# Sparse attention's paired score products in one chain, two PSUM banks at a time, and both sums of values behind all scores

## The chip, the cores and the metric

The kernel runs on one core of a Trainium2 chip. The metric is the device time of one execution in microseconds (us), the median of several runs. TensorE (PE) multiplies matrices, VectorE (DVE) and ScalarE (ACT) work on elements and empty PSUM, GpSimd (POOL) does a little, and SyncE (SP) issues the transfers.

## The reference, cut to what matters

One layer of a streaming encoder block over 256 frames of 1024 channels: a combined input projection, two attention branches, gates, an output projection, a residual sum, a mixture of experts, a norm. The branch that the change touches is the sparse attention: an indexer picks 64 keys for each query, and attention runs over these. The kernel computes the scores over all keys and adds a bias of -1e30 where a key was not picked.

```python
def indexed_sparse_attention(q, k, v, q_idx, k_idx, w_idx, top_k):
    ...
    score = jnp.einsum('bqh,bqhk->bqk', wi, jax.nn.relu(logits))
    _, sel = lax.top_k(jnp.where(adm[None], score, -jnp.inf), top_k)
    k_sel, v_sel = gather(k, sel), gather(v, sel)
    s = jnp.einsum('bqhd,bqkhd->bhqk', qi, k_sel) * (DSA_HEAD_DIM ** -0.5)
    p = jax.nn.softmax(jnp.where(sel_ok[:, None], s, NEG), axis=-1)
    return jnp.einsum('bhqk,bqkhd->bqhd', p, v_sel)
```

Eight heads of 64 channels; queries in two blocks of 128 (`j` = 0, 1), with 128 and 256 keys.

## The kernel before

Every fp32 product is made of three products of fp32r halves (`hi`, `lo`): `mm3` (L301 to L303) for operands that fill 128 rows, `mm3_pair` (L318) for operands of 64 rows. `mm3_pair` is given two sets of operands, one in partitions 0 to 63 and one in partitions 64 to 127, and issues them by turns, each into a bank of its own.

The work comes in stages. The input projections and the indexer fill the first 118 us or so; `select` (L473) is the indexer's score, which uses `mm3_pair` too. Then come the attention branches, as generators that are advanced by hand (`steps`): `attend` for the latent attention and `attend_pairs` (L604) for the sparse one, in two quads of four heads, `B[0]` and `B[1]`. One advance of `attend_pairs` is one block of queries: two banks of scores are taken from `psS`, each is opened by a product that adds the bias (L615) and gets six products (L318) from each of two heads' halves; then, bank by bank, the row maximum (DVE L623), the exponentials (ACT L629), a reciprocal and a scaling (DVE L632, L634), transposes on PE (L640) and a copy into `PT` (ACT L642, L644). The third advance sums the values: 16 products (L652) into one bank of `psS`, and its evacuation by ACT L291 and DVE L294 into `obT`.

`psS` has two banks in all; each `pss()` takes the one that comes free. `psA` (four banks) holds the projections, `psT` (two banks) the transposes.

The order in which an engine runs its instructions is worked out when the kernel is built, by a planner that simulates all engines with a table of costs and takes, of what is ready, what has the highest priority. `steps` raises the priority of the attention's instructions by 400 places. Beside them stand the gates' and output projections, `project_late` (L725): 4 slabs' worth of splits into halves (`split_late`, ACT L282 or L297 and DVE L283 or L297) and the products L301 to L303 on them. `halves` holds four split parts. `after(i, j)` adds an edge to the planner: `i` comes behind `j` in the program of their engine. It makes no instruction.

Weights come by `issue` (L215) in SP's queue, attention slabs (`w_att`) through a ring of four places, and expert slabs (`w_moe`, 96 of 1 MB) into every place that has come free, such as those of `PT`, of `vb` and of `obT`. The experts begin with a gather (L895) and `gate_up` (L1047) and take the slabs in order; a slab's place is loaded again when its products are done.

Of the kernel before, what the change touches and what calls it, by code (L numbers as in the profile page):

```python
# [78 lines left out]
def block_kernel(ctx: ExitStack, tc: tile.TileContext, a, out, cap=CAP):  # L79
    nc = tc.nc  # L80
# [9 lines left out]
    def after(i, j):  # L90
        tc.add_manual_dep(i.ins, j.ins.name, nosync, reason="the latter goes first")
# [15 lines left out]
    def at(place, shape, dt=F32R, name="r"):  # L107
        n = int(np.prod(shape[1:]))
        t = rp.tile([128, 2048], dt, tag=place,
                    name=name)  # L110
        return shaped(t[:, :n], shape)
# [6 lines left out]
    def pt(name="t", which=None):  # L118

        if which is None:  # L120
            which = t_turn[0] = 1 - t_turn[0]
        return psT.tile([128, 512], F32, tag=f"t{which}", name=name)

    def pss(name="s"):
        return psS.tile([128, 512], F32, tag="s", name=name)

    def bc(ap, n, axis=1):

        p, m = ap.shape
        return ap[:, None, :].to_broadcast([p, n, m]) if axis == 1 else ap[:, :, None].to_broadcast([p, m, n])  # L130
# [37 lines left out]
    ident_r = cp.tile([128, 128], F32R, name="ident_r")  # L168
# [121 lines left out]
    def evac(hi, lo, ps, place=None):  # L290
        i = nc.scalar.copy(hi, ps)  # L291
        if place:
            first[place] = i.ins
        return i, nc.vector.tensor_sub(lo, ps, hi.bitcast(F32))  # L294
# [16 lines left out]

    row_halves = slice(0, 64), slice(64, 128)

    def mm3_pair(both, start, stop):

        for l, r, s0, s1 in ((1, 3, start, False), (1, 4, False, False), (2, 3, False, stop)):
            for ops in both:
                nc.tensor.matmul(ops[0], ops[l], ops[r], start=s0, stop=s1)  # L318

    scr_turn = [0]  # L320

# [113 lines left out]
    bias = wk.tile([128, 2, 256], F32R, tag="b3", name="bias", bufs=1)  # L435
# [37 lines left out]
    def select(j):  # L473

        nk = 128 * (j + 1)
        per = 512 // nk
        qs = slice(j * 128, (j + 1) * 128)
        sc = e0[:, 1664:1920] if j else e0[:, 1536:1664]
        for h0 in range(0, 4, per):
            p = [pss() for _ in range(2)]  # L480
            for i in range(per):
                mm3_pair([(p[z][:, i * nk:(i + 1) * nk], qiT[ps_, 0, h0 + i, qs], qiT[ps_, 1, h0 + i, qs],
                           kiT[ps_, 0, :nk], kiT[ps_, 1, :nk]) for z, ps_ in enumerate(row_halves)], True, True)
            for z in range(2):
                rl = wk.tile([128, 512], F32, tag="b2", name="rl", bufs=3)
                nc.scalar.activation(rl, p[z], AF.Relu)
                for i in range(per):
                    h = 4 * z + h0 + i
                    nc.vector.scalar_tensor_tensor(sc, rl[:, i * nk:(i + 1) * nk], wi[:, j, h:h + 1],
                                                   adm[:, 256 - nk:] if h == 0 else sc, op0=ALU.mult, op1=ALU.add)  # L490
        for r in range(TOPK // 8):
            m8 = wk.tile([128, 8], F32, tag="m8", name="m8")
            nc.vector.max(out=m8, in_=sc)
            nc.vector.match_replace(out=sc, in_to_replace=m8, in_values=sc, imm_value=TAKEN)
        nc.vector.tensor_scalar(bias[:, j, :nk], sc, -2e38, NEG, op0=ALU.is_gt, op1=ALU.mult)
# [66 lines left out]
    def attend(quad, scores, v, oT, op):  # L562
# [38 lines left out]
        evac(oT[:, 0, 2 * quad:2 * quad + 2], oT[:, 1, 2 * quad:2 * quad + 2], o.rearrange("p (c q) -> p c q", c=2), op)  # L601
        yield

    def attend_pairs(quad, v, oT, op):  # L604


        turn[0] = 1 - turn[0]
        place = f"T{turn[0]}"
        PT = at(place, [128, 4, 3, 128], F32)
        for j in range(2):  # L610
            nk = 128 * (j + 1)
            qs = slice(j * 128, (j + 1) * 128)
            p = [pss()[:, :2 * nk] for _ in range(2)]
            for z in range(2):
                nc.tensor.matmul(p[z].rearrange("p (h k) -> p h k", h=2), ident_r, bc(bias[:, j, :nk], 2), start=True,  # L615
                                 stop=False)
            for i in range(2):
                h = 2 * quad + i
                mm3_pair([(p[z][:, i * nk:(i + 1) * nk], qbT[r, 0, h, qs], qbT[r, 1, h, qs], kbT[r, 0, h, :nk],
                           kbT[r, 1, h, :nk]) for z, r in enumerate(row_halves)], False, i == 1)  # L620
            for z in range(2):
                nm = wk.tile([128, 4], F32, tag="nm", name="nm")[:, :2]
                nc.vector.tensor_reduce(nm, p[z].rearrange("p (h k) -> p h k", h=2), axis=AX.X, op=ALU.max, negate=True)  # L623
                if j or not z:
                    P = wk.tile([128, 512], F32, tag="b2", name="P", bufs=3)
                Pz = P[:, 256 * z:256 * z + 256] if j == 0 else P
                sm = wk.tile([128, 4], F32, tag="sm", name="sm")[:, :2]
                for i in range(2):
                    nc.scalar.activation(Pz[:, i * nk:(i + 1) * nk], p[z][:, i * nk:(i + 1) * nk], AF.Exp,  # L629
                                         bias=nm[:, i:i + 1], scale=1.0, accum_out=sm[:, i:i + 1])  # L630
                rs = wk.tile([128, 4], F32, tag="rs", name="rs")[:, :2]
                nc.vector.reciprocal(rs, sm)  # L632
                for i in range(2):
                    nc.vector.tensor_scalar(Pz[:, i * nk:(i + 1) * nk], Pz[:, i * nk:(i + 1) * nk], rs[:, i:i + 1], None,  # L634
                                            op0=ALU.mult)
                if z == 0 or j:
                    tp = pt()
                for b in range(2 * (j + 1)):
                    c = 256 * z + 128 * b if j == 0 else 128 * b
                    nc.tensor.transpose(tp[:, c:c + 128], P[:, c:c + 128], ident)  # L640
                if j:
                    nc.scalar.copy(PT[:, 2 * z:2 * z + 2, 1:3], tp.rearrange("p (h b q) -> p h b q", h=2, b=2))  # L642
                elif z:
                    first[place] = nc.scalar.copy(PT[:, :, 0], tp.rearrange("p (h q) -> p h q", h=4)).ins  # L644
            yield
        o = pss("o")
        for c in range(2):
            for b in range(2):
                for i in range(2):
                    r = slice(64 * i, 64 * i + 64)  # L650
                    h = 2 * quad + 4 * c + i
                    nc.tensor.matmul(o[r, c * 256 + 128 * b:(c + 1) * 256], v[:, b, 64 * h:64 * h + 64],  # L652
                                     PT[:, 2 * c + i, 0:2] if b == 0 else PT[:, 2 * c + i, 2], start=b == 0, stop=b == 1)
        evac(oT[:, 0, quad::2], oT[:, 1, quad::2], o.rearrange("p (c q) -> p c q", c=2), op)
        yield

    def steps(g, n):
        with tc.high_priority(400):
            for _ in range(n):
                next(g, None)  # L660
# [47 lines left out]
    qbT = at("C0", [128, 2, 4, S])  # L708
# [5 lines left out]
    kbT = at("C1", [128, 2, 4, S])  # L714
    dsa_heads(acc, kbT, 0, "C1")
    steps(A[1], 1)
    obT = at("C1", [128, 2, 4, S])
    B = [attend_pairs(quad, vb, obT, "C1") for quad in range(2)]
    steps(B[0], 2)
    steps(B[1], 1)  # L720
    steps(B[0], 1)
    steps(B[1], 2)


    def project_late(nslabs, lhs, banks, g=None):  # L725
# [446 lines left out]
    with in_order, tc.manual_schedule(engines={mybir.EngineType.Activation, mybir.EngineType.DVE}):  # L1172
        for grp in range(NG):
# [26 lines left out]
            if grp + 1 < NG:  # L1200
                for c in range(2):
                    p = pss("gx")
# [128 lines left out]
```

## Time and profile before

| | us |
|---|---|
| median of 3 runs | 427.56 |
| lowest, highest | 427.43, 428.58 |
| profiled execution, its own time | 428.7 |
| profiled execution, span of the instructions | 426.9 |

The span runs from the first to the last instruction of the profiled execution; 1.8 us of its time lie outside. In a timeline an instruction's duration runs to its modelled end, so that pipelined products overlap and the distance between two starts is what each costs. The mean granted clock of TensorE over the span is 0.972 of its upper level, 2.4 GHz.

### The profile page before, as it was taken

What the parts mean: (1) busy time and instruction counts of PE and PEld (TensorE: products, weight loads), DVE (VectorE), ACT (ScalarE), POOL (GpSimd) and SP (SyncE); (2) the same over time, 40 slices, a digit from 0 to 9 for tenths busy, and PEclk for the clock granted to TensorE, in tenths of its full rate; (3) what the DMA queues carried; (4) which work ended last, traced back from release to release, by engine and by line L of the source; (5) the groups of instructions that cost most, each with busy time, mean ns of one, the idle gap of its engine ahead of it and who ended that gap; (6) DMA issues with size and microseconds to landing.
All of it is one profiled execution on the core that took longest, in us unless ns stands there. A gap on an engine that the chain in (4) does not pass through costs nothing.

```text
span 426.9 us, 8162 instructions
## 1 busy us (share of the span) xinstructions
PE 400.3 (94%) x3288; PEld 292.6 (69%) x3288; DVE 205.8 (48%) x546; ACT 185.2 (43%) x403; POOL 27.7 (6%) x30
## 2 busy tenths in 40 slices
PE   7999999999999999999999999999999797788780
PEld 4888887888877787888886757575757373364440
DVE  2889689989857474757572222121213011020023
ACT  3876688578856665565442122221221111111142
POOL 0890000000000000000001010101010001000000
PEclk9999999999999999999999999999999889698996
DMA  7995673648553464978885999999999999999962
GB/s 264 395 338 194 256 296 129 264 164 332 198 188 128 161 253 176 378 284 341 334 321 184 418 421 421 421 418 420 420 421 419 421 419 421 422 418 420 417 253 104
DMA packets 20639, 135.00 MB, mean 316 GB/s; under 512 B 2418, under 2 KB 2930, under 8 KB 5620
## 3 DMA queue, kind: packets, MB, share of 16 engines
q1 hardware_dynamic: 20596, 134.42, 79.3%
q8 instruction: 28, 0.46, 0.4%
q14 instruction: 15, 0.12, 0.1%
HBM read 133.36 MB, written 1.05 MB: 315 GB/s over the span
## 4 chain that ended last, share of the span: by engine, by line
PE 77%; DMA 19%; DVE 2%; issue 0%; ACT 0%; SPq 0%; DVEq 0%
DMA w<-in_w_moe 18%; PE a L301 13%; PE a L302 13%; PE a L303 13%; PE G L1047 9%; PE gx L895 5%; PE Y L1088 5%; PE OA L1102 3%; PE G L1063 3%; PE s L318 2%; PE o L599 1%; DMA x<-in_x 1%; PE t L640 1%; PE t L539 1%; PE o L652 1%; PE t L451 1%
## 5 line engine op out<-in xcount | busy, mean ns | idle before, releaser
L302 PE MATMUL a<-r 128*128 128x512 f32 (+1 forms) x244 | 93.9, 387 | 0.0
L303 PE MATMUL a<-r 128*128 128x512 f32 (+1 forms) x244 | 92.1, 383 | 0.0
L301 PE MATMUL a<-r 128*128 128x512 f32 (+1 forms) x244 | 84.6, 390 | 0.0
L1047 PE MATMUL G<-w,tok 128*32 128x256 f32 x1024 | 71.2, 406 | 11.6 <-DMA w<-in_w_moe 11.4
L297 DVE SCALAR_TENSOR_TENSOR r<-w,ident,r 128x512 fp32r<-128x512 f32 (+2 forms) x79 | 62.4, 803 | 13.1 <-ACT r L297 12.7
L297 ACT ACTIVATE r<-w,ident 128x512 fp32r<-128x512 f32 (+2 forms) x79 | 57.0, 751 | 24.5 <-PE a L303 22.7
L1047 PEld LDWEIGHTS G<-w,tok 128*32 128x32 f32 x1024 | 30.0, 114 | 38.8 <-issue 15.8
L302 PEld LDWEIGHTS a<-r 128*128 128x128 f32 x244 | 45.9, 188 | 8.7 <-DVE r L297 0.3
L301 PEld LDWEIGHTS a<-r 128*128 128x128 f32 x244 | 45.4, 189 | 9.3 <-ACT r L291 0.5
L303 PEld LDWEIGHTS a<-r 128*128 128x128 f32 x244 | 45.8, 188 | 8.1
L1069 DVE TENSOR_TENSOR P<-G,P 128x64 f32<-128x64 f32 x32 | 7.2, 225 | 82.9 <-ACT P L1068 82.9
L1068 ACT ACTIVATE P<-G 128x64 f32<-128x64 f32 x32 | 7.2, 224 | 73.6 <-PE G L1063 73.6
L1088 PE MATMUL Y<-w,P 128*32 128x256 f32 x512 | 31.0, 382 | 2.2 <-DMA w<-in_w_moe 2.2
L1053 ACT COPY Gs<-G 128x256 f32<-128x256 f32 x32 | 11.9, 372 | 48.8 <-PE G L1047 48.8
L895 PEld LDWEIGHTS gx<-Pr,x 128*128 128x128 f32 x256 | 29.2, 192 | 3.3 <-issue 2.9
L297 DVE SCALAR_TENSOR_TENSOR ysb<-Y,ws,ysb 128x512 fp32r<-128x512 f32 (+1 forms) x18 | 12.5, 692 | 38.8 <-ACT ysb L297 19.6
L895 PE MATMUL gx<-Pr,x 128*128 128x128 f32 x256 | 30.7, 278 | 0.2 <-DVE Pr L880 0.2
L283 DVE TENSOR_TENSOR r<-w,r 128x512 fp32r<-128x512 f32 x32 | 21.9, 690 | 17.3 <-ACT r L282 15.7
L880 POOL TENSOR_SCALAR Pr<-P,r 128x128 f32<-128x128 f32 x14 | 8.3, 606 | 320.2 <-PE gx L895 195.1
L282 ACT CAST r<-w 128x512 fp32r<-128x512 f32 x32 | 19.8, 622 | 15.0 <-PE a L303 8.3
L1063 PEld LDWEIGHTS G<-cst,Gs 128*128 128x128 f32 x128 | 17.5, 199 | 9.8 <-issue 5.3
L1088 PEld LDWEIGHTS Y<-w,P 128*32 128x32 f32 x512 | 15.1, 109 | 12.6 <-DMA w<-in_w_moe 2.5
(223 smaller groups left out, 463.0 us busy)
## 6 DMA issues: line engine op xcount, KB each, us to landing
w<-in_w_moe SPq DMA_DIRECT2D x93, 1024.0 KB, 19.8
w<-in_w_att SPq DMA_DIRECT2D x24, 1024.0 KB, 4.9
w<-in_w_moe SPq DMA_DIRECT2D x6, 512.0 KB, 15.0
w<-in_w_att SPq DMA_DIRECT2D x3, 744.0 KB, 8.4
w<-in_w_att SPq DMA_DIRECT2D x2, 512.0 KB, 5.3
out<-r SPq DMA_DIRECT2D x2, 512.0 KB, 3.5
w<-in_w_att SPq DMA_DIRECT2D x1, 768.0 KB, 6.0
w<-in_w_att SPq DMA_DIRECT2D x2, 372.0 KB, 6.0
```

Of the source, the lines that this page charges most:

```text
L282: nc.scalar.copy(hi, src)
L283: nc.vector.tensor_sub(lo, src, hi.bitcast(F32))
L297: return nc.scalar.mul(hi, ps, g), nc.vector.scalar_tensor_tensor(lo, ps, g, hi.bitcast(F32), op0=ALU.mult, op1=ALU.subtract)
L301: i = nc.tensor.matmul(out_, lh, rh, start=start, stop=False)
L302: nc.tensor.matmul(out_, lh, rl, start=False, stop=False)
L303: nc.tensor.matmul(out_, ll, rh, start=False, stop=stop)
L895: nc.tensor.matmul(p[:, kk * GRP:(kk + 1) * GRP], x2[:, t, k * 128:(k + 1) * 128], Pr[:, t], start=(t == 0 and kk == 0), stop=(t == 1 and ...
L1047: nc.tensor.matmul(G[quarters[2 * z + o], :256], tokens[c][:, kk + o, CAP * e:CAP * e + CAP], w[:, (kk + o) * 512 + z * 256:(kk + o) * 512 ...
L1053: nc.scalar.copy(Gs, G[:, :256])
L1063: nc.tensor.matmul(HT[:, f * 64:(f + 1) * 64], Gs[:, f * 128:(f + 1) * 128], fold, start=True, stop=True)
L1088: nc.tensor.matmul(Y[quarters[e]], hT_[:, e, f], wv[:, f, e], start=f == 0, stop=f == 1)
L1102: nc.tensor.matmul(OA[t][h][:, c0:c0 + w], pl[:, t * 128:(t + 1) * 128], v, start=False, stop=grp == NG - 1 and q0 > 0 and v is lo, skip_g ...
```

## The change

`mm3_pair` puts each product that it issues behind the one before, and returns the last. In `attend_pairs` the first of these is put behind the second bank's bias product, the second head's products behind the first head's, and a pair's first bias product behind the last product of the pair before (`paired`). `select` calls `mm3_pair` without a start, so there the six products of one call are chained among themselves. The advances of the two quads are put into another order: before B0, B0, B1, B0 (sum), B1, B1 (sum), after B0, B0, B1, B1, B0 (sum), B1 (sum).

```diff
-    def mm3_pair(both, start, stop):
+    def mm3_pair(both, start, stop, behind=None):
 
         for l, r, s0, s1 in ((1, 3, start, False), (1, 4, False, False), (2, 3, False, stop)):
             for ops in both:
-                nc.tensor.matmul(ops[0], ops[l], ops[r], start=s0, stop=s1)
+                i = nc.tensor.matmul(ops[0], ops[l], ops[r], start=s0, stop=s1)
+                if behind:
+                    after(i, behind)
+                behind = i
+        return behind
...
+    paired = []
+
     def attend_pairs(quad, v, oT, op):
...
             for z in range(2):
-                nc.tensor.matmul(p[z].rearrange("p (h k) -> p h k", h=2), ident_r, bc(bias[:, j, :nk], 2), start=True,
-                                 stop=False)
+                i_ = nc.tensor.matmul(p[z].rearrange("p (h k) -> p h k", h=2), ident_r, bc(bias[:, j, :nk], 2), start=True,
+                                      stop=False)
+                if not z and paired:
+                    after(i_, paired.pop())
             for i in range(2):
                 h = 2 * quad + i
-                mm3_pair([(p[z][:, i * nk:(i + 1) * nk], qbT[r, 0, h, qs], qbT[r, 1, h, qs], kbT[r, 0, h, :nk],
-                           kbT[r, 1, h, :nk]) for z, r in enumerate(row_halves)], False, i == 1)
+                i_ = mm3_pair([(p[z][:, i * nk:(i + 1) * nk], qbT[r, 0, h, qs], qbT[r, 1, h, qs], kbT[r, 0, h, :nk],
+                           kbT[r, 1, h, :nk]) for z, r in enumerate(row_halves)], False, i == 1, i_)
+            paired.append(i_)
...
     steps(B[0], 2)
+    steps(B[1], 2)
+    steps(B[0], 1)
     steps(B[1], 1)
-    steps(B[0], 1)
-    steps(B[1], 2)
```

## Rows read from the trace of the kernel before

**Rows 1.** The page of the profile: busy time of the engines (us, share of the span, instructions), and two lines of the span in 40 equal slices (PE busy in tenths, DMA engines busy in tenths).

```profile
PE 400.3 (94%) x3288; PEld 292.6 (69%) x3288; DVE 205.8 (48%) x546; ACT 185.2 (43%) x403; POOL 27.7 (6%) x30
...
PE   7999999999999999999999999999999797788780
...
DMA  7995673648553464978885999999999999999962
```

**Rows 2.** Stretches of the span: the stretch and its length in us, busy us (and instructions) of PE, of weight loads, DVE, ACT and POOL, the granted clock of TensorE, the busy share of the DMA engines, GB/s.

```profile
150.00:160.00 10.00, 10.00 (x49) 8.10 (x48) 7.72 (x15) 6.51 (x13) 0.00 (x0) 1.00 0.65 242
160.00:170.00 10.00, 9.98 (x54) 7.14 (x53) 4.51 (x7) 6.30 (x10) 0.00 (x0) 1.00 0.51 181
188.00:222.00 34.00, 34.00 (x187) 28.93 (x186) 22.66 (x61) 17.27 (x35) 0.00 (x0) 1.00 0.92 356
222.00:228.00 6.00, 5.84 (x61) 4.79 (x63) 4.44 (x22) 1.10 (x6) 1.21 (x2) 1.00 0.05 19
...
230.00:328.00 98.00, 98.00 (x1244) 66.59 (x1247) 20.64 (x59) 20.82 (x55) 4.75 (x8) 1.00 1.01 418
328.00:407.00 79.00, 65.25 (x696) 38.46 (x684) 10.28 (x29) 12.55 (x32) 2.38 (x4) 0.89 1.01 419
```

**Rows 3.** The chain that ended last, in order of time, from 320 us to the end: start, us, what.

```profile
328.45 19.94 DMA w<-in_w_moe
...
388.24 18.66 DMA w<-in_w_moe
```

**Rows 4.** Waits of SP's queue between 160 and 245 us: who waited for whom, us in total, times, the longest.

```profile
SPq L215 <- PE G L1047: 18.7, 7, 11.7
...
SPq L215 <- PE o L652: 6.6, 1, 6.6
```

**Rows 5.** The chain over the whole span, its paired products in `select`: start, us from the first start to what comes next, count.

```profile
59.76 1.26 PE s L318 x20
65.56 0.91 PE s L318 x12
```

**Rows 6.** The chain between 118 and 170 us, the same products in `attend_pairs`.

```profile
124.24 0.81 PE s L318 x6
126.29 0.81 PE s L318 x6
...
129.38 0.91 PE s L318 x6
...
131.36 0.91 PE s L318 x6
137.82 0.81 PE s L318 x6
139.02 0.81 PE s L318 x6
...
147.03 0.79 PE s L318 x5
...
154.47 0.90 PE s L318 x6
```

**Rows 7.** Timeline of PE, the borders of such blocks: start, us to the modelled end, line, operation, tiles and shape, count.

```profile
128.76 0.39 PE L303 MATMUL a<-r 128*128 128x512 f32 x1
128.98 0.40 PE L615 MATMUL s<-bias,ident_r 128*128 128x512 f32 x1
129.31 0.98 PE L318 MATMUL s<-r 64*128 64x256 f32 x6
...
132.20 0.50 PE L302 MATMUL a<-r 128*128 128x512 f32 x1
132.54 0.40 PE L303 MATMUL a<-r 128*128 128x512 f32 x1
132.78 0.39 PE L302 MATMUL a<-r 128*128 128x512 f32 x1
...
145.86 0.49 PE L615 MATMUL s<-bias,ident_r 128*128 128x512 f32 x1
146.28 0.38 PE L318 MATMUL s<-r 64*128 64x256 f32 x1
146.59 0.44 PE L652 MATMUL o<-r 128*64 128x128 f32 x4
146.96 0.86 PE L318 MATMUL s<-r 64*128 64x256 f32 x5
```

**Rows 8.** Timeline of DVE and of ACT between 124 and 146 us, the softmax of the bank whose products end at 132.27: its row maximum, and the last of its exponentials.

```profile
132.31 0.69 DVE L623 TENSOR_REDUCE nm<-s 128x2 f32<-128x512 f32 x1 [0.15 <-PE s L318]
...
134.58 0.46 ACT L629 ACTIVATE P<-s,nm 128x256 f32<-128x256 f32 x1
```

**Rows 9.** Waits of all engines between 110 and 235 us, one row: ACT's splits of weights waiting for PE.

```profile
ACT r L297 <- PE a L303: 10.0, 15, 1.4
```

**Rows 10.** Timeline of ACT between 168 and 187 us: the evacuation of the last sum of values, and the first split of the slab that is multiplied with `obT`.

```profile
168.69 0.59 ACT L291 CAST r<-o 128x512 fp32r<-128x512 f32 x1 [0.52 <-PE o L652]
...
181.46 0.62 ACT L282 CAST r<-w 128x512 fp32r<-128x512 f32 x1 [0.33 <-PE a L303]
```

**Rows 11.** Timeline of SP's queue, two issues behind the last sum of values.

```profile
168.68 0.33 SPq L215 DMA_DIRECT2D w<-in_w_moe  x1
169.11 0.38 SPq L215 DMA_DIRECT2D w<-in_w_att  x1
```

## Prediction, written before the changed kernel was run

> **What bounds the kernel now.** I read the page first. PE is busy for 94% of the span, in tenths 9 in nearly every slice to about 330 us; the DMA engines are half idle until about 220 us and full from there to 410 us [rows 1]. An average over two such halves says little, so I cut the span into stretches [rows 2]. Up to 222 us PE is never free: 10.00 of 10 us, 34.00 of 34. From 230 us the DMA engines are at 1.01 and move 418 GB/s, while PE is full to 328 us and then only 65 of 79 us. The chain that ended last says the same of the end: from 328.45 to 406.90 us it consists of expert slabs' transfers [rows 3].
>
> The kernel is thus bound by PE first and by the transfers afterwards, and what couples the two decides what a gain on PE is worth. Between 222 and 228 us the DMA engines do almost nothing (share 0.05) [rows 2], and SP's queue stands in its longest wait of that part, 11.7 us, for the first `gate_up` products, L1047 [rows 4]. All places are full then; the stream of expert slabs starts again only when PE has used up the first of them. From that moment nothing but bytes stands between it and the end. So a microsecond that PE saves before 222 us starts the stream a microsecond earlier and ends the kernel a microsecond earlier, as long as the prefetch before is done in time. It has slack: it ends about 6 us ahead of the restart, and is busy for 0.92 of 188 to 222 us and 0.51 to 0.65 of 150 to 170 us [rows 2].
>
> The change works between 118 and 170 us, on PE's bound side.
>
> **Pairing.** Two places of the trace show the same products in two orders. In `select` the two row halves alternate: 12 products of 256 columns take 0.91 us, 20 of 128 columns 1.26 us [rows 5]. In `attend_pairs` they don't: each bank is opened by its own bias product, gets its six products, and the other bank follows 1 to 8 us later, with other work between. There six products of 256 columns take 0.91 us and six of 128 columns 0.81 us [rows 6]. Twelve alternating products cost what six of one half cost, so the two halves of the array work at once when they are fed by turns. For 128 columns the same follows from the steps: 20 products are 10 steps in 1.26 us, six of one half are 6 steps in 0.81 us, a step is (1.26 - 0.81) / 4 = 0.11 us, and 12 alternating products, 6 steps, take 0.81 us. The chain of the change forces the turns: z = 0, z = 1, z = 0, and so on, behind both bias products. Each of the four pairs of blocks then becomes one block, and the second of each goes: 0.81 + 0.91 + 0.81 + 0.90 = 3.43 us [rows 6].
>
> **Borders.** A block of 64-row products costs something on entry and exit. A full product starts 0.22 to 0.24 us after the one before, but from the bias product at 128.98 to the block behind it are 0.33 us, and from the first product behind a block, 132.20, to the next are 0.34 us [rows 7]. That is 0.10 us at each border, and four blocks fewer make eight borders fewer: 0.8 us.
>
> **The split block.** B1's first 256-column block was cut: one product at 146.28, four sums of values at 146.59, then the other five [rows 7]. Its first product alone takes 0.31 us, against 0.11 us for a step in a block; with the sums traced behind all scores this cut has no reason to happen: 0.2 us. The other sums are moved, not removed; their price is the same wherever they stand, and I take nothing for them.
>
> **The chain in `select`.** The six products of a call get edges in the order that they already show: its blocks of 20 and 12 run at the paired price [rows 5]. I take nothing; if one more cut came in or one went, it would be two borders, 0.2 us either way. The edges make no instructions.
>
> **What can be lost.** The planner may put other work between the links of a chain. Transposes of an earlier bank (L640) have the priority of earlier work and can become due in the middle of a pair. Such a cut costs two borders and perhaps a lone product, 0.2 to 0.4 us; with none to two in each pair it is 0 to 3.2 us. Blocks in the trace are mostly whole (seven of eight) [rows 6], so I take one cut in all, 0.2 us.
>
> **The waits that are added.** A pair now needs both banks of `psS` at its start. A bank is free when its softmax has read it: for the block that ends at 132.27 us the row maximum starts at 132.31 and the last exponential ends at 135.04 us [rows 8], 2.8 us. In PE's queue stands, behind a pair that waits, everything else of PE. What hides this is the projections: between the blocks that end at 132.27 and begin at 137.82 us [rows 6] PE had products L301 to L303 to do, and these are enough for any place that the planner chooses. I cost it at nothing, with an upper end of 2.8 us for each of the three pairs that follow another, 8.4 us, if nothing were put between.
>
> Behind this stands a second cover. Two softmaxes now come in one burst, and ACT and DVE also split the weights for PE. ACT waited for PE 15 times, 10.0 us in all, with its next split [rows 9], so it runs ahead. Four split parts are kept, each worth six products of 0.23 us, 1.4 us: 5.5 us of cover against a burst of about 2.8 us. Nothing, again; without that cover PE would miss the difference of the burst, at most 2.8 us a pair.
>
> One rule of the Trainium skill speaks against the change here: TensorEngine Tiling (Array Packing), section Performance Considerations, says that tiling speeds up TensorE but not the emptying of PSUM, which can become the bottleneck. By that rule the pairs would come no faster than the 2.8 us of the softmax let them; by the rows that price is covered, and the sum stands.
>
> **What is late next.** The sums of values move behind all scores. B0's sum, in part at 146.59 us before [rows 7], comes later; `PT`'s place then takes an expert slab later. B1's scores end earlier, since its last block no longer waits for B0's sum to leave a bank, so `obT` should not be later than now: it is evacuated from 168.69 us, and the slab that is multiplied with it is split from 181.46 us [rows 10], a slack of 12 us. On SP's queue a slab of attention weights can stand behind an expert slab that waits for a place. It did before: the queue waited 6.6 us for L652 [rows 4], the attention slab behind followed at 169.11 us [rows 11], and PE was still busy for 9.98 of those 10 us [rows 2]. So I cost the moved issues at nothing.
>
> **The sum.** 3.43 + 0.8 + 0.2 - 0.2 = 4.2 us off PE's stage, all of it before 170 us, and passed on whole. Span 426.9 - 4.2 = 422.7; with the 1.8 us outside it, 424.5 for an execution like the profiled one (428.7). That one lies 1.1 us above the median of the runs, so the forecast for the median is 427.56 - 4.2 = 423.4 us. Its own range is 422.6 to 424.5.
>
> **Rivals.**
>
> *Cuts.* The pairs are alternated, but transposes and sums break them up, or the two bias products and the pair stand apart. One or two cuts a pair of 0.2 to 0.4 us leave 1.6 to 3 us of gain: 424.6 to 426.0. For it: the cut block at 146.28, and that edges don't forbid other work between. Against it: seven whole blocks of eight, and 20 and 12 in one piece in `select`. Chance 0.18.
>
> *Order elsewhere.* The planner's later order changes for the better beyond my sum, such as fewer cuts of the sums of values: 421 to 422.5. Chance 0.04.
>
> *Nothing arrives.* PE waits for second banks or splits about 1.4 us before each of three pairs and loses what it gains, or the change's edges don't keep the turns on the chip: 427.6, within 0.3%. For it: the planner's costs aren't the chip's, and PE takes its queue in order. Against: no stretch between 118 and 222 us shows PE free [rows 2]. Chance 0.12.
>
> *Slower.* The banks. The planner puts a pair directly where its simulation has both banks free, the chip frees the second up to 2.8 us later, and PE stands with all projections behind it. Three times 2.8 us less the gain of 4.2 us is 4.2 us slower: 431.8. It decides from a mean wait of 1.4 us before the three pairs. For it: both banks of `psS` are in every pair, so no bank is left to work ahead in; against it: softmax times are regular, and PE met no such wait with the same two banks before. Chance 0.11. By the skill page named above this is the case to expect whenever evacuation is the slower side; the trace agrees only in that 2.8 us are more than the 0.9 us of a block.
>
> **From these to the numbers.** The forecast has 0.55. From no change, a measurement of this kernel can tell about 0.3%, 1.3 us. Faster by more: 0.55 + 0.18 + 0.04 = 0.77; within: 0.12; slower: 0.11. The range leaves out the slower case, about half of the case without change and half of the large gains, 0.19 in all: 421.8 to 427.4.
>
> **What would show it.** In the changed trace, L318 in four blocks of 12, 0.81 us for 128 columns and 0.91 us for 256, each behind two bias products; no idle PE before L615 or L318; the restart of the expert stream behind L1047 about 4 us earlier than 228 us, with DMA share 1.01 after it; the last expert transfer at about 402.7 instead of 406.90 us. Blocks of 4 or 8 with other lines between would be the first rival, PE idle before L615 the last. The forecast is wrong in its coupling if PE's stage is 4 us shorter and the stream's restart or its length doesn't follow.

## The result, and the profile after

The changed kernel takes 423.26 us, the median of 4 runs (422.87 to 424.31), against 427.94 us (427.43 to 428.58) for the kernel before beside it: a ratio of 0.9893, 95% interval 0.987 to 0.9915, or 3.6 to 5.6 us off. The forecast was 423.4 us. A second series of the same kernel gave 424.01 us and 0.9916 (0.9889 to 0.9942). The profiled execution took 422.87 us with a span of 421.1 us.

The page of the changed kernel, its lines for busy time and for the DMA engines over the span:

```profile
PE 391.6 (93%) x3288; PEld 287.8 (68%) x3288; DVE 205.3 (49%) x546; ACT 184.1 (44%) x403; POOL 27.0 (6%) x30
...
DMA  7995673748544489679867999999999999999962
```

Against [rows 1] PE has as many products and is busy for 8.7 us less; that is more than the change gains, for it counts the start and the end too, where the two executions differ (65.25 against 63.65 us in the last row of the two tables of stretches). Stretches of the span in which the work is about that of [rows 2], each some 4 us earlier (columns as there):

```profile
184.00:218.00 34.00, 33.89 (x188) 28.53 (x186) 23.42 (x67) 16.07 (x32) 0.00 (x0) 1.00 0.90 341
218.00:224.00 6.00, 5.96 (x73) 4.88 (x77) 3.41 (x16) 1.29 (x7) 1.21 (x2) 1.00 0.16 37
226.00:324.00 98.00, 98.00 (x1238) 66.56 (x1235) 20.64 (x59) 20.74 (x55) 4.75 (x8) 1.00 1.01 421
324.00:403.00 79.00, 63.65 (x701) 37.69 (x699) 10.45 (x31) 12.55 (x34) 2.38 (x4) 0.94 1.01 419
```

The structure is the same: PE full, a pause of the transfers around 220 us, then transfers at 1.01 to the end. SP's queue, in its waits from 156 to 241 us, still waits longest for the first `gate_up` products, now L1056, again 11.7 us; its wait for a sum of values (L661, 6.6 us before [rows 4]) is down to 2.7 us:

```profile
SPq L215 <- PE G L1056: 19.2, 8, 11.7
...
SPq L215 <- PE o L661: 2.7, 1, 2.7
```

The place of the gain. PE's products stand in the same order in both kernels up to about 120 us, `select` included, so the two executions can be laid over each other at a point ahead of the change: the first pair of the second latent sum. The timeline of PE has it in the kernel before

```profile
119.58 0.65 PE L599 MATMUL o<-r 128*64 128x256 f32 x2
```

and in the changed kernel

```profile
118.68 0.65 PE L603 MATMUL o<-r 128*64 128x256 f32 x2
```

The chain of the kernel before has the experts' gather, the stage's end, at

```profile
223.22 3.84 PE gx L895 x32
227.05 2.73 PE G L1047 x48
```

and the chain of the changed kernel, with `select`'s paired products of [rows 5] as its first row and the expert transfers of [rows 3] as its last two:

```profile
58.85 1.26 PE s L318 x20
...
218.04 3.84 PE gx L904 x32
221.88 2.73 PE G L1056 x48
...
319.97 19.80 DMA w<-in_w_moe
...
382.24 18.66 DMA w<-in_w_moe
```

From these rows the difference of the two spans, 5.8 us, splits up. 0.91 us are there already at 58.85 against 59.76 us, in products that the change left in their order. They arise in the first 14 us, where PE's first products took longer in the execution of before: five products of zeros (L374, in the changed kernel L378) 2.34 us against 1.24. Why is not settled. PE's stage takes 223.22 - 119.58 = 103.64 us before and 218.04 - 118.68 = 99.36 us after, 4.28 us less: this is the change. From the first `gate_up` to the last transfer it is 406.90 - 227.05 = 179.85 and 400.90 - 221.88 = 179.02 us, 0.83 us less. This last part is not the change's either: in the second series the changed kernel itself took 179.9 us there. Behind the last transfer the changed kernel's execution is about 0.2 us longer. So the two spans lie 1.5 us further apart than the stages, and the medians, 4.7 us apart, or 3.8 us in the second series, agree with a stage that is 4.28 us shorter. In what follows I go by this stage, which came out within 0.05 us in two executions of one kernel (99.36 and 99.32, and 98.83 and 98.80 for another), and by the runs' medians behind it.

The chain between 122 and 150 us shows the pairs, to be read against [rows 6]:

```profile
124.75 0.81 PE s L318 x12
128.77 0.92 PE s L318 x12
136.99 0.82 PE s L318 x12
144.79 0.43 PE s L318 x3
145.59 0.79 PE s L318 x8
```

Twelve products for 0.81 and 0.92 us where six took 0.81 and 0.91 us. The last pair is cut, and the timeline shows by what: two transposes of an earlier bank (one of the nine products behind them falls outside the chain's row). It also shows the borders, that is, what it costs to go from full products to 64-row products and back, as [rows 7] did:

```profile
128.29 0.48 PE L621 MATMUL s<-bias,ident_r 128*128 128x512 f32 x1
128.70 0.98 PE L318 MATMUL s<-r 64*128 64x256 f32 x12
129.62 0.50 PE L302 MATMUL a<-r 128*128 128x512 f32 x1
129.95 0.40 PE L303 MATMUL a<-r 128*128 128x512 f32 x1
...
144.72 0.50 PE L318 MATMUL s<-r 64*128 64x256 f32 x3
145.15 0.44 PE L649 MATMUL t<-ident,P 128*128 128x128 f32 x2
145.52 0.86 PE L318 MATMUL s<-r 64*128 64x256 f32 x9
```

Summed over the stage, from each product's start to the next one's, by kind of product (the remaining kinds agree within 0.01 us):

| | before, us | after, us | difference |
|---|---|---|---|
| paired products, 128 columns, 24 | 3.25 | 1.63 | -1.61 |
| paired products, 256 columns, 24 | 3.82 | 2.14 | -1.68 |
| bias products, 8 | 2.51 | 2.22 | -0.30 |
| products of projections, 316 | 74.31 | 73.74 | -0.56 |
| sums of values, 48 | 5.53 | 5.08 | -0.45 |
| transposes of `P` and of heads, 48 | 4.72 | 5.05 | +0.33 |

### The profile page after: what moved, and what is told of

Same layout as the page of the kernel before. It is cut to its first block, busy times and chain, and to the rows that moved or that the text cites. A ratio compares the mean times of both kernels' runs of the same rounds, so it can differ in the third digit from the quotient of the medians.

```text
span 421.1 us, 8166 instructions
## 1 busy us (share of the span) xinstructions
PE 391.6 (93%) x3288; PEld 287.8 (68%) x3288; DVE 205.3 (49%) x546; ACT 184.1 (44%) x403; POOL 27.0 (6%) x30
## 4 chain that ended last, share of the span: by engine, by line
PE 75%; DMA 20%; DVE 2%; ACT 1%; issue 0%; SPq 0%; DVEq 0%; ACTq 0%
DMA w<-in_w_moe 19%; PE a L301 13%; PE a L302 13%; PE a L303 13%; PE G L1056 9%; PE gx L904 5%; PE Y L1097 5%; PE OA L1111 3%; PE G L1072 3%; PE s L318 2%; DMA w<-in_w_att 1%; PE o L603 1%; PE t L543 1%; PE t L649 1%; PE o L661 1%; PE t L455 1%
## 5 line engine op out<-in xcount | busy, mean ns | idle before, releaser
L1056 PE MATMUL G<-w,tok 128*32 128x256 f32 x1024 | 68.5, 394 | 12.1 <-DMA w<-in_w_moe 12.1
L1056 PEld LDWEIGHTS G<-w,tok 128*32 128x32 f32 x1024 | 29.2, 111 | 37.8 <-issue 14.0
L909 DVE TENSOR_TENSOR tok<-gx,ident 128x512 f32<-128x512 f32 x16 | 11.1, 692 | 27.1 <-PE gx L904 26.9
```

Source lines behind the costliest of these rows:

```text
L1056: nc.tensor.matmul(G[quarters[2 * z + o], :256], tokens[c][:, kk + o, CAP * e:CAP * e + CAP], w[:, (kk + o) * 512 + z * 256:(kk + o) * 512 ...
```

## The experiments

My theory: PE gains where the two row halves take turns in its queue, the rest are borders, and the gain passes one to one to the end through the restart of the expert stream. The rivals: the order of the advances gains, not the chain; the standing together gains, not the turns; the transfers have an end of their own.

**The new order without the chain.** The kernel before, with only the last hunk of the diff:

```diff
     steps(B[0], 2)
+    steps(B[1], 2)
+    steps(B[0], 1)
     steps(B[1], 1)
-    steps(B[0], 1)
-    steps(B[1], 2)
```

> The kernel before with the new order of advances alone, no chain. Theory (turns): the gain of the change comes from the two row halves alternating, which needs the chain; the order by itself leaves the banks one after the other and takes off only the cut of the sums of values, so 427.4 to 427.9 us, and PE's stage from the first sum of the latent attention to the experts' gather 0 to 0.5 us shorter than the 103.6 us of before. Rival (order): the sums of values moved behind the scores are what gains; then about 423.5 us and a stage of about 99.5 us without any chain.

426.38 us against 427.90 us, ratio 0.997 (0.9957 to 0.9982), and a stage of 221.21 - 118.34 = 102.87 us, 0.77 us shorter. More than I had expected (0 to 0.5 us, and 427.4 us or more), far less than the change. The timeline of its PE shows why the two can't be told apart cleanly at the last pair:

```profile
143.58 0.50 PE L318 MATMUL s<-r 64*128 64x256 f32 x2
...
144.38 0.38 PE L318 MATMUL s<-r 64*128 64x256 f32 x1
144.69 0.49 PE L615 MATMUL s<-bias,ident_r 128*128 128x512 f32 x1
145.11 0.50 PE L318 MATMUL s<-r 64*128 64x256 f32 x2
...
145.91 0.74 PE L318 MATMUL s<-r 64*128 64x256 f32 x7
```

With the sum of values out of the way both banks come free together here, and the planner starts the second one while the first has three products left. The other three pairs stay blocks of six. The sums of values, whole again, are 0.45 us cheaper, which is the whole amount of the table above. The projections are 0.50 us cheaper here too, of the table's 0.56, and the transposes, which cut the last pair, 0.35 us dearer: these differences come with the order and not with the chain.

**The chain in the old order.** In the kernel before, `obT` lies in the place C1, and so do the keys `kbT`. The timeline of its ACT shows what that does to the sum of B0, whose products end at 148.6 us:

```profile
155.40 0.59 ACT L291 CAST r<-o 128x512 fp32r<-128x512 f32 x1 [0.36 <-PE s L318]
```

The sum can't leave its bank before the last scores have read the keys. A pair that needs both banks behind that sum would wait for itself; read from the code, the old order and the chain exclude each other while the sums go to C1. So the chain was tried in the old order with another place for them:

```diff
-    obT = at("C1", [128, 2, 4, S])
-    B = [attend_pairs(quad, vb, obT, "C1") for quad in range(2)]
+    obT = at("S2", [128, 2, 4, S])
+    B = [attend_pairs(quad, vb, obT, "S2") for quad in range(2)]
     steps(B[0], 2)
-    steps(B[1], 2)
-    steps(B[0], 1)
     steps(B[1], 1)
+    steps(B[0], 1)
+    steps(B[1], 2)
```

> The changed kernel with the old order of advances (B0, B0, B1, sum of B0, B1, sum of B1); so that this can be run, the sums go to the place S2 instead of C1, which they share with the keys. Theory (turns): four blocks of 12 alternating products as in the changed kernel, stage 99.4 to 100.0 us, time 423.0 to 424.0 us. Rival (order): 427 us or more, stage about 103 us.

423.83 us, ratio 0.990 (0.9877 to 0.9922), stage 218.55 - 119.02 = 99.53 us, in four whole blocks of 12: all but 0.17 us of the gain. The control, the kernel before with that place and nothing else:

> The kernel before with the sums of values in the place S2 instead of C1, and nothing else; the control for the run with the old order and the chain. Theory: PE's blocks stay at six products, stage 103.2 to 103.8 us, time 427.3 to 428.2 us. Rival (the place was what held the banks): 1 us or more faster.

427.34 us, ratio 0.9987 (0.9973 to 1.0001), stage 222.47 - 119.05 = 103.42 us, blocks of six but for the split one, as before. So the chain takes 3.89 us off the stage in the old order (103.42 to 99.53) and 3.51 us in the new one (102.87 to 99.36); the new order takes 0.77 us by itself and, as far as the code tells, is what makes the chain possible in the places given.

**Together, but without turns.** Both banks' bias products first, then six products of one half and six of the other, in one chain:

```diff
-            for i in range(2):
-                h = 2 * quad + i
-                i_ = mm3_pair([(...) for z, r in enumerate(row_halves)], False, i == 1, i_)
+            for z, r in enumerate(row_halves):
+                for i in range(2):
+                    h = 2 * quad + i
+                    i_ = mm3_pair([(...)], False, i == 1, i_)
```

> The changed kernel with both banks' products in one uninterrupted chain, but six of one half first and then six of the other. Theory (turns): a step without a partner costs what a pair costs, 0.11 us, so four blocks get six steps longer each: 24 x 0.11 = 2.7 us, to 3.4 us if the change of half costs a border; stage 102.1 to 102.8 us, time 426.0 to 426.7 us. Rival (borders): what gains is that twelve products stand together and PE changes its mode less often; then the stage stays at 99.4 to 99.8 us and the time at 423.3 us.

424.13 us, ratio 0.9908 (0.9888 to 0.9929), stage 219.35 - 119.03 = 100.32 us: 0.96 us more than with turns, where I had expected 2.7 to 3.4 us. The rival's 99.4 to 99.8 us is missed too, from the other side. The chain of this kernel between 123 and 147 us has the blocks:

```profile
125.10 1.10 PE s L318 x12
...
129.38 1.25 PE s L318 x12
...
137.23 1.09 PE s L318 x12
```

By the steps of the shorter products, twelve of 0.11 us one after the other, with what a block has beside its steps, would be 1.49 us (an estimate: 0.81 us and six more steps); six are 0.81 us. 1.10 us is 2.6 steps more than six, 1.25 against 0.92 us is 2.9. The second half thus begins beside the first when that has about three products left to start, although six stand ahead of it in the queue. The single records of the first block bear it out: its third and fourth product start 7 ns apart, at 125.304 and 125.311 us, where products of one half stand 0.11 us apart. A record doesn't name the half; that the fourth is the other half's first is read from the distances. My theory of turns falls in this form: by this reading PE doesn't stop at a product whose half is busy, it goes past it to products for the other half, by about three.

**Turns of three.** The test of that reading:

```diff
             for i in range(2):
                 h = 2 * quad + i
-                i_ = mm3_pair([(...) for z, r in enumerate(row_halves)], False, i == 1, i_)
+                for z, r in enumerate(row_halves):
+                    i_ = mm3_pair([(...)], False, i == 1, i_)
```

> The changed kernel with the halves alternating in threes (three products of one half, three of the other, and so on) instead of one by one. In the run of six and six, twelve products took 1.09 us (128 columns) and 1.25 us (256) and the second half began beside the third or fourth product of the first. Theory (PE runs ahead of a product that waits for its half by about three products): threes cost 0 to 0.1 us a block more than turns of one, 0.81 to 0.91 and 0.91 to 1.0 us, stage 99.4 to 99.8 us. Rival (each change of half costs a step): four runs of three, 1.1 us or more a block, stage over 100.3 us.

423.74 us, ratio 0.9905 (0.9882 to 0.9928), stage 218.06 - 118.56 = 99.50 us, 0.14 us more than with turns of one. Its chain:

```profile
124.63 0.82 PE s L318 x12
128.60 0.92 PE s L318 x12
136.87 0.82 PE s L318 x12
```

A run of three costs nothing in these three blocks; the 0.14 us are for the most part at the last pair, which is cut in another place.

**A known delay ahead of the experts.**

```diff
-    heat(lgp[0], 6)
+    heat(lgp[0], 36)
```

> The changed kernel with 30 more idle products on PE (128x256, about 0.138 us each by the 14 that stand there already) among the router's logits, ahead of the experts: a known delay of 30 x 0.138 = 4.1 us on PE before the expert stream restarts. Theory (coupling one to one): restart 4.1 us later, time 427.4 us. Rival (the transfers have slack or a floor of their own): less than 2 us later, 425 us or less.

425.72 us, ratio 0.9956 (0.9937 to 0.9975), between the theory's 427.4 and the rival's 425. The timeline of PE, with the 36 idle products and the gather:

```profile
215.08 4.09 PE L310 MATMUL s<-ident_r 128*128 128x256 bf16 x36
...
221.34 3.74 PE L904 MATMUL gx<-Pr,x 128*128 128x128 f32 x32
```

Six of them took 0.82 us in the changed kernel, so 30 add 3.27 us, 0.11 us each and not 0.138 (the 14 before contain borders). The stage is 221.34 - 119.20 = 102.14 us, 2.78 us longer; the rest fell into small waits that stood there. The last transfer ends at 404.02 us, 284.82 us behind the common point, against 282.22 us: 2.60 us of 2.78 arrive. Against the second profiled execution of the changed kernel (283.03 us) only 1.79 us do, and the medians lie 1.7 to 2.5 us apart. One such pair therefore settles no more than that most of the delay arrives. Firmer is the length of the transfers' part over all thirteen kept traces: from the first `gate_up` to the last transfer's end it is 178.9 to 180.0 us, whether PE's stage ahead of it takes 98.8, 102.1 or 103.6 us, and 179.1 us in the kernel below whose stage is 15 us longer. The coupling is one to one within the 1 us or so by which executions differ.

**The same work in the transfers' part.**

```diff
                 if grp == NG - 1 and e:
-                    heat(idle_bank, HEAT)
+                    heat(idle_bank, HEAT + 5)
```

at both places in the last group's loop over experts.

> The changed kernel with 30 more idle products on PE, the same 4.1 us of work, spread over the last group of experts, where PE waits for transfers. Theory: the stream alone sets the end there, so 0 to 0.5 us, 423.2 to 423.8 us. Rival (PE's work counts wherever it stands): 427 us.

423.49 us, ratio 0.9891 (0.9858 to 0.9923): nothing that the runs can tell, as expected, and 2.2 us less than with the same products ahead of the experts. The 30 products, from 387 us on in its trace, are free where they stand.

**The cover taken away.** The late projections' first products are put behind the last pair:

```diff
-                    mm3(banks[t], lh[:, k, ts], ll[:, k, ts], hi, lo, k == 0, k == total - 1)
+                    i = mm3(banks[t], lh[:, k, ts], ll[:, k, ts], hi, lo, k == 0, k == total - 1)
+                    if k == 0:
+                        after(i, paired[-1])
```

> The changed kernel with the products of the late projections kept behind the last pair of scores, so that nothing covers the waits for the softmax between pairs. Theory (cover): PE then stands before three pairs until both banks are empty, 2.8 us each by the trace of before and up to 4 us where two softmaxes come in one burst: 8 to 12 us of idle PE between 120 and 145 us, time 431 to 436 us. Rival (the banks empty fast enough by themselves): less than 3 us, 426 us or less.

438.79 us, ratio 1.0261 (1.0225 to 1.0296), worse than the 436 us of my upper end. The timeline of PE shows the waits for the softmax ahead of bias products, and two pairs:

```profile
116.46 0.50 PE L621 MATMUL s<-bias,ident_r 128*128 128x512 f32 x1 [1.42 <-ACT P L638]
...
121.92 0.38 PE L621 MATMUL s<-bias,ident_r 128*128 128x256 f32 x1 [1.55 <-ACT P L638]
...
123.14 1.03 PE L318 MATMUL s<-r 64*128 64x128 f32 x12
...
127.50 1.65 PE L318 MATMUL s<-r 64*128 64x256 f32 x12
```

and the stretches show what came on top (granted clock in the third column from the end):

```profile
90.00:100.00 10.00, 8.46 (x59) 7.04 (x57) 9.96 (x32) 5.69 (x15) 0.00 (x0) 1.00 0.91 372
100.00:110.00 10.00, 7.76 (x49) 5.93 (x49) 8.49 (x31) 7.35 (x24) 0.00 (x0) 0.83 0.51 183
110.00:120.00 10.00, 7.05 (x50) 4.79 (x48) 4.86 (x14) 3.84 (x12) 0.00 (x0) 0.85 0.44 165
120.00:130.00 10.00, 8.15 (x42) 5.64 (x41) 5.29 (x18) 4.91 (x20) 0.00 (x0) 0.67 0.00 1
130.00:140.00 10.00, 10.00 (x58) 7.83 (x57) 5.64 (x12) 7.20 (x17) 0.00 (x0) 0.97 0.46 152
```

The waits themselves are 1.4 to 1.6 us, half of what I had allowed, and stand before two of the three pairs that follow another. But the edit does more than was meant: the latent attention ahead loses the same cover. PE is free for 1.54 and 2.24 us in the first two stretches, at a granted clock of 1.00 and then 0.83, and for 2.95 and 1.85 us in the next two, where the clock is 0.85 and 0.67 on average, between its two levels (1.2 and 2.4 GHz); the pair at 127.50 us takes 1.65 us where it took 0.98. In all PE is free for 8.6 us between 90 and 130 us, against 0.1 us in the changed kernel, and 5.3 us of that lie ahead of the first pair's scores. The other 6 us or so of the 15 lie in slower products; what the waits of the pairs alone would have cost was not measured.

**The cut taken out.** The pairs' products get a higher priority, so that transposes that become due wait for the pair's end:

```diff
-            for i in range(2):
-                h = 2 * quad + i
-                i_ = mm3_pair(...)
+            with tc.high_priority(150):
+                for i in range(2):
+                    h = 2 * quad + i
+                    i_ = mm3_pair(...)
```

> The changed kernel with the pairs' products 150 places higher in priority, so that transposes don't cut the last pair (cut behind its third product at 144.72 us in the changed kernel). Theory: one cut less, two borders of 0.1 us and a lone product: stage 0.2 to 0.4 us shorter than 99.4 us, and no difference in time that can be measured, 422.6 to 423.4 us. Rival (cuts are dear): 1 us or more faster.

422.52 us, ratio 0.9869 (0.985 to 0.9887), stage 217.53 - 118.70 = 98.83 us, 0.53 us shorter where I had expected 0.2 to 0.4. The last pair in its chain is whole, 0.90 us:

```profile
144.81 0.90 PE s L318 x12
```

Because this is the version that would beat both, it and the changed kernel were run once more on one chip.

> The changed kernel once more, beside the next ones on the same chip: 422.9 to 424.3 us, PE's stage from the first sum of the latent attention to the experts' gather 99.4 us.

> The changed kernel with the pairs' products 150 places higher in priority, once more: the stage was 98.8 us against 99.4 us. If that is what the cut costs, 0.5 us less than the changed kernel beside it; if the 0.7 us between their medians came from the chips, no difference.

424.01 us (0.9916) and 422.93 us (0.9868, 0.9844 to 0.9892), stages 99.32 and 98.80 us. The cut costs 0.53 and 0.52 us in the stage: 0.32 us in the paired products and 0.17 us in transposes. The medians lie 0.7 and 1.1 us apart in the same direction; by time alone their intervals overlap, by the stage the difference is plain.

## Why the prediction was right

**Bound and coupling: right.** The stage is 4.28 us shorter, the first `gate_up` starts 5.17 us earlier in a trace whose start was 0.91 us earlier, and DMA share is 1.01 behind it. The last transfer ends at 400.90 us, not at 402.7; the differences of the executions account for it. Of the 2.78 us put in ahead of the experts 1.8 to 2.6 came out at the end, of the same work in the tail nothing, and the transfers' part is as long behind a short stage as behind a long one.

**Pairing: the size right, the mechanism too narrow.** 3.43 us were forecast from whole blocks, and 0.2 us more from the split block, whose lone product belongs to the same rows of the table: 3.63 us without a cut. The two kernels without one, the last above and the chain in the old order, show 3.62 us; with its cut the changed kernel shows 3.29 us. But the sentence that the halves work at once "when they are fed by turns" asks for too much. It took the order that the trace of `select` happened to show for the condition. Without any turns, two thirds of this gain stay (the paired products of the six-and-six kernel take 4.80 us in the stage, against 7.06 before and 3.77 with turns), and turns of three are as good as turns of one. Nor does PE, by those runs, take its queue strictly in order, as one rival there says. What the change had to bring, and brought, is that both halves' products stand within a few places of each other in PE's queue.

**Borders: too high.** 0.8 us were forecast for the chain. Where the chain alone is the difference, all but the paired products give 0.4 us (the new order without it and the changed kernel) and 0.3 us (the old order with the sums in S2, without and with it). A single border was read rightly at 0.10 us, but not each comes back. The second bias product of the pair at 128.70 us stands behind two transposes now, and 0.41 us pass from it to the pair where 0.33 did; and behind the transposes at 122.67 us PE waits some 0.2 us for an evacuation, which the first block used to fill.

**The sums: put at nothing, which was wrong.** Their price was taken to be "the same wherever they stand". It isn't: each is one run of 16 now, the sums are 0.45 us cheaper, and the projections beside them are 0.5 us cheaper as well, by the run of the new order alone. With 0.16 us at the pairs, and 0.35 us more for transposes, the order by itself was worth 0.77 us of the stage, where 0.2 us, those of the split block, were forecast.

**The cut: right in number, low in price.** One cut was assumed at 0.2 us; one came, and its removal is worth 0.52 us of the stage, 0.32 us of them in the pairs.

**Waits and cover: right that they cost nothing, wrong in two readings.** No wait of PE for a bank shows in the stage. Uncovered, a wait is 1.4 to 1.6 us, not 2.8; the idle time in the latent attention and the fall of the clock, neither of which I had priced, make the uncovered case worse than my rival of 431.8 us all the same. And B1's last block did not wait "for B0's sum to leave a bank": the sum waited for the last scores, since `obT` and `kbT` share a place, which the prediction didn't follow. It didn't touch the forecast's sum, but, as far as the code tells, it is why the chain and the order of the advances come together.

Side by side: 3.29 us at the pairs, the split block and the cut included (forecast 3.43), and 0.98 us at all the rest of the table (0.8): 4.27 against 4.23 us. Behind the second figure stand two errors of about half a microsecond, borders of 0.3 to 0.4 us where 0.8 were forecast, and 0.6 us from the order outside the pairs where nothing was. They cancel; that the total fits to 0.05 us is luck in these terms, while the largest, the pairing, was right by itself.

The rule on emptying PSUM that was weighed before, from the Trainium skill (TensorEngine Tiling (Array Packing), section Performance Considerations, where the copy may become the bottleneck after a fourfold speedup), shows in the kernel without cover: PE waits 1.42 and 1.55 us for the softmax. With the projections between, the trace shows no such wait.

## What to carry to other kernels

In these traces products of 64 rows overlap when those of the two halves stand close together in PE's queue; a planner that gives each bank its own moment loses that, and its trace shows it as n products of one half in the time in which 2n could run. Before such products are tied together, look at what each bank waits for on its way out, down to the place in memory that its evacuation writes. And measure a change of this size on a stage that begins and ends at the same products in both traces: here it repeats within 0.05 us, where two medians of one kernel lie up to 0.75 us apart. A part with a control of its own tells more than a total that fits: here the total fitted while two of its terms did not.

## What the runs showed of the hardware

By the distances of the starts, PE starts products for a free row half past about three products that wait for the busy one: twelve products queued six and six took 1.09 to 1.10 us at 128 columns and 1.25 us at 256, between 0.81 and 0.92 us for six steps and the 1.49 us estimated for twelve of 128 columns in a row. Sixty-four-row products of one half start every 0.11 to 0.12 us whether they have 128 columns or 256: six take 0.81 or 0.91 us [rows 6], so the shorter ones gain little by being short. A border between these and full products of 512 columns costs 0.10 us each way (0.33 and 0.34 us from start to start, where 0.22 to 0.24 are usual [rows 7]), but 0.41 us stood at one entry whose bias product came behind transposes. The transfer part from the first `gate_up` to the last landing came out at 179.0 or 179.9 us in two executions of the changed kernel, and at 178.9 or 179.9 us in two of the one without a cut, which no change here explains.
